# Second-half forms of x written over the used inputs of the output projection, and one combined first step of the feed-forward

## The chip, the cores and the metric

The kernel runs on one core of one Trainium2 chip. The metric is the device time of one execution in microseconds (us), the median of the runs; lower is better. Engines are named as in the profile: PE is the matmul engine (TensorE), PEld its weight loads, DVE the vector engine, ACT the scalar engine, POOL is GpSimd, and SP issues the DMAs.

## The reference

One inference step of a two-layer streaming encoder over 1088 frames (1024 of a new stream, 64 of a running one) with a model width of 1024. Per layer:

```python
h = rms_norm(x, norm_mix_g[layer])
y = even_mixer(h, ...) if layer % 2 == 0 else odd_mixer(h, ...)   # ends in concat(two branches) @ w_out
x = x + y
h = rms_norm(x, norm_ffn_g[layer])
x = x + jnp.square(jax.nn.relu(h @ w_ff1[layer])) @ w_ff2[layer]  # 1024 -> 4096 -> 1024
```

Layer 0 mixes by chunk gating (branch a) and trailing pooling (branch b), layer 1 by a width-31 convolution (branch c) and a gated width-3 convolution (branch d). At the end there is one more rms_norm. All of it is float32.

## The kernel before

Activations lie transposed: x is eight tiles of 128 features by 1088 frames. Every float32 operand of a product is split into a high part (a rounded copy made by ACT, line 165) and a low part (what is left, subtracted by DVE, line 166), and a product is three matmuls: low weight by high data, high by low, high by high. The frames are handled in two halves, c = 0 and c = 1, of 544 frames each, and a half in two quarters of 272.

The two products of the feed-forward are done by a scheme with seven sub-products instead of eight. For it, both the weights and the data are turned into seven **forms** (sums and differences of blocks, each split into a high and a low part). Weight forms are made by `form` (lines 207, 212, then the split) in six buffers W, up to five ahead of their use. Forms of x for one half are made by `forms_of_x` for four row blocks k from x[k] and x[k+4]: two scaled copies on ACT (line 703), five small DVE operations of 272 columns (lines 708, 709, 688, and one split), and three splits of 544 columns. Those of the first half go into the tiles FA, those of the second half into FB.

`last_parts` is the second part of the output projection for one half. For eight tiles m in the order 0, 4, 1, 5, 2, 6, 3, 7 it runs 24 or 48 matmuls (lines 257 to 259), adds the product to x on DVE (line 743), squares x on ACT (line 752) and adds the square to acc on POOL (line 753). With it run steps from the list `beside`, the forms of x among them. For c = 0 they follow their tile; for c = 1 they are collected in `later` and come after the last tile, because FB lies on the side of the memory that still holds the inputs of the output projection (Q, or cc in layer 1): `open_second` gives that side free and takes FB and four work tiles vl from it.

The first product of the feed-forward (`feed_forward`, lines 819 to 821 in `products`) has 16 blocks i of weights. The list STEPS1 takes blocks 0 and 1 for the half c = 0, then blocks 0 and 1 for c = 1, and then each block from 2 to 15 for both halves at once. Each entry of the list is planned with weight forms of its own, so the forms of blocks 0 and 1 are made twice. A step sums its seven sub-products in three pairs of banks (A, B, C; four pairs pp in all): after f = 0, 1, 2 ACT copies a bank out (line 862), after f = 3, 4, 5 DVE adds one (line 865) and scales it (line 858), and after f = 6 DVE scales the last (line 858). The results go to DRAM (hd, line 853) and are read back as forms for the second product (class `Hidden`, line 837). The sum of the result into x is line 901. The order on every engine is set by a scheduler at build time.

Of the kernel before, what the change touches and what calls it, by code (L numbers as in the profile page):

```python
# [11 lines left out]
F32 = mybir.dt.float32  # L12
# [4 lines left out]
P = 128  # L17
# [39 lines left out]
def encoder(ctx, tc, ins, outs):  # L57
# [29 lines left out]
    RIGHT = {"P1", "P2", "t", "raw", "FA", "vr", "sq", "RAW", "e", "cin", "dd", "wide", "r2"}  # L87
    LEFT = {"Q1", "Q2", "FB", "vl", "cc"}

# [14 lines left out]
    def q2(dt=F32R, n=T):  # L104
        return sb([P, n], dt, "Q2", 8)

# [5 lines left out]

    def vl(n=NH):
        return sb([P, n], F32, "vl", 4)

# [222 lines left out]

    STEPS1 = [(0, (0,)), (1, (0,)), (0, (1,)), (1, (1,))] + [(i, (0, 1)) for i in range(2, 16)]


# [9 lines left out]
    def plan_ff(layer):  # L351
        plan(f"f{layer}", None, "stage")
        for s, (i, _) in enumerate(STEPS1):
            src = ins[f"wf1_{layer}"][i].rearrange("p (b c) -> p b c", b=4)
            for f in range(7):
                plan(("f1", layer, s, f), src, "form")
# [65 lines left out]
    for i in range(4):  # L422
        wv.append((q2(n=1024), q2(n=1024)))
        split(*wv[i], wvr[i])
        if i == 0:
            gains(x0[0], *PIECES[0])
# [183 lines left out]
    def pool_out(g, pp):  # L610
        yb[g] = (q2(), q2())
# [17 lines left out]


    ya = []

    def u_tile(m):
        w = take(("u", m))
        ya.append((q1(), q1()))
        for c, (a, b) in enumerate(CH):
            ps = psum()
            n = b - a
            mm3(ps[:, :n], unit_pairs(w, h, c, range(KT)))
            if between and c == 0:  # L640
                between.pop(0)()
            u = tmp()
            dve.tensor_tensor(u[:, :n], ps[:, :n], acc[:, a:b], ALU.mult)
            act.activation(u[:, :n], u[:, :n], AF.Gelu_apprx_tanh)
            dve.tensor_tensor(mix[m][:, a:b], mix[m][:, a:b], u[:, :n], ALU.mult)
            split(ya[m][0][:, a:b], ya[m][1][:, a:b], mix[m][:, a:b])

# [25 lines left out]
    def open_first():  # L673

        open_side("right")
        state["form"] = True
        for k in range(4):
            FF[0, k] = sb([P, 7, 2, NQ], F32R, "FA", 4)

    def open_second():  # L680
        open_side("left")
        vl()
        for k in (3, 2, 0, 1):
            FF[1, k] = sb([P, 7, 2, NQ], F32R, "FB", 4)

# [4 lines left out]
    def forms_of_x(layer, k, c):  # L690
# [5 lines left out]
        def put(f, n, src):  # L696
            t = FF[c, k][:, f : f + n]
            split(t[:, :, 0], t[:, :, 1], src)
# [7 lines left out]
        def first():  # L706
            y1, y2, u, w = b
            dve.tensor_tensor(u[:, 0], y1[:, 0], y1[:, 1], ALU.subtract)
            dve.tensor_tensor(w[:, 0], y2[:, 1], y1[:, 1], ALU.subtract)
            put(0, 1, y1[:, 0:1])  # L710

        def second():
# [8 lines left out]

        return [gains_, first, second, third, lambda: put(5, 2, b[3])]


    def add_out(m, c, w, t, ks):
        a = c * NH
        ps = pair()
        for i in range(2):
            o = a + i * NQ
            mm3(  # L730
                ps[:, i, :NQ],
                [
                    (
                        w[0][:, q * P : (q + 1) * P],
                        w[1][:, q * P : (q + 1) * P],
                        t[0][k][:, o : o + NQ],
                        t[1][k][:, o : o + NQ],
                    )
                    for q, k in ks
                ],  # L740
            )
# [13 lines left out]
    def last_parts(layer, c, weights, t, ks):  # L755

        later = []
        for m in MS:
# [7 lines left out]
        beside.extend(later)  # L766

    load_x(ins["xT"])
    open_psum("f0", 4)
    open_first()  # L770
    begun.add("f0")
    mixed = [t[0] for t in ya + yb], [t[1] for t in ya + yb]
    last_parts(0, 0, lambda m: take(("o0", m)), mixed, [(k, k) for k in (4, 5, 6, 7, 0, 1, 2, 3)])
    for i, m in enumerate(MS):
        add_out(m, 1, take(("o0b", m), 5), mixed, [(k - 4, k) for k in range(4, 8)])
        if i == 1:
            rms_half(0, vr())
    last_parts(0, 1, lambda m: take(("o0a", m), 5), mixed, [(k, k) for k in range(4)])

# [4 lines left out]
    def feed_forward(layer, done):  # L784
# [7 lines left out]

        open_second()
# [4 lines left out]
        def products(key, cs, n, rows):  # L798

# [3 lines left out]
            bank = {}  # L803
            for f, (name, first) in enumerate(
                (("A", True), ("B", True), ("A", False), ("C", True), ("A", False), ("B", False), ("A", False))
            ):
                if first:
                    bank[name] = pair()
                if (*key, f) not in kept:
                    kept[(*key, f)] = take((*key, f), 5)  # L810
                w = kept[(*key, f)]
                for c in cs:
                    ps = bank[name][:, c, :NQ]
                    for q in range(n):
                        lh, ll = w[:, 0, q * P : q * P + P], w[:, 1, q * P : q * P + P]
                        t = FF[c, rows(q, c)][:, PLACE[f]]
                        hi, lo = t[:, 0], t[:, 1]
                        s, e = first and q == 0, q == n - 1
                        pe.matmul(ps, ll, hi, start=s, stop=False, skip_group_check=True)  # L819
                        pe.matmul(ps, lh, lo, start=False, stop=False, skip_group_check=True)  # L820
                        pe.matmul(ps, lh, hi, start=False, stop=e, skip_group_check=True)  # L821
                yield f, bank[name][:, cs[0] : cs[-1] + 1, :NQ]
                aside(2)


        def place(i, c):
            return (3, 2, 0, 1)[i % 4] if c else i % 4

        class Hidden:
# [5 lines left out]
            def form(self, f):  # L835
                t = self.buffer()
                dma.dma_start(out=t, in_=hd[self.i][f])
                for c in range(2):
                    to = FF[c, place(self.i, c)][:, PLACE[f]]
                    split(to[:, 0], to[:, 1], t[:, c * NQ : c * NQ + NQ])  # L840

        factor = acc.rearrange("p (c h t) -> p c h t", c=2, h=2)
        for s, (i, cs) in enumerate(STEPS1):
            last = Hidden(0, vr) if s == len(STEPS1) - 1 else None
            if s == 2:
                aside(len(beside))
            z = {k: halves(vl() if last or s < 2 else vs()) for k in (0, 3, 1, 2)}
            for f, ps in products(("f1", layer, s), cs, 4, lambda q, c: q):
                v = {k: t[:, cs[0] : cs[-1] + 1] for k, t in z.items()}
# [28 lines left out]
                if f == 6:  # L878
# [15 lines left out]
        for j, lo, hi, make, cs in STEPS2 + ENDS[layer]:  # L894
            nxt = [Hidden(i) for i in make]
            part = slice(cs[0], cs[-1] + 1)
            for f, ps in products(("f2", layer, (j, lo)), cs, hi - lo, lambda q, c: place(lo + q, c)):

# [22 lines left out]

    h1 = [[[None] * KT for _ in range(2)] for _ in range(2)]

    def after(j, cs):
        t = sb([P, 7, NH], F32R, "FB", 4)
        places = [t[:, i] for i in range(7)] + [sb([P, NH], F32R, "vl", 4)]

# [215 lines left out]

    cc, means = [], {}


    def ln_steps(c):
# [36 lines left out]
        def finish_(j):  # L1184
            dve.tensor_tensor(ct[j], ct[j], st["r"], ALU.mult)
            act.activation(ct[j], ct[j], AF.Silu, scale=col(O_LG + j), bias=col(O_LB + j))
            split(cc[j][0][:, a:b], cc[j][1][:, a:b], ct[j])

# [9 lines left out]

    open_side("left")
    cc.extend(tuple(sb([P, T], F32R, "cc", 8) for _ in range(2)) for _ in range(4))  # L1200
    load_x(xd)
    dh = [t[0] for t in dd], [t[1] for t in dd]
    for m in MS:
# [8 lines left out]
    begun.add("f1")  # L1212
    mixed = [t[0] for t in cc], [t[1] for t in cc]
    last_parts(1, 0, lambda m: take(("o1c", 0, m), 5), mixed, [(k, k) for k in range(4)])
# [129 lines left out]
```

## Time and profile before

| | |
|---|---|
| median of 3 runs | 2109.45 us (2108.42 to 2110.8) |
| the profiled execution | 2106.23 us, its span 2104.4 us |
| granted clock of PE, mean | 0.983 of full speed |
| PE busy | 2004.5 us (95%) |
| PEld busy | 1969.6 us (94%) |
| DVE busy | 1653.7 us (79%) |
| ACT busy | 965.4 us (46%) |
| POOL busy | 261.5 us (12%) |

PE is busy 95% of the span. In long stretches it never waits; the rest is lost in a few places, mostly at the borders of the stages. So the shares of the whole span say little here, and the profile has to be read by stretches of time and by single waits.

### The profile page before, as it was taken

How to read it: one execution, taken by the hardware profiler on the slowest of the kernel's cores; microseconds unless marked ns; L12 is line 12 of the kernel's file. 1: busy time of each engine (PE TensorE's matmuls, PEld its weight loads, DVE VectorE, ACT ScalarE, POOL GpSimd, SP SyncE). 2: the span in 40 equal slices, each digit the busy share in tenths (PEclk: the TensorE clock that was granted, in tenths of full speed). 3: DMA queues.
4: the chain of work that ended last, by engine and by line, in shares of the span. 5: the costliest groups of instructions: out<-in, count | busy, mean ns of one | idle time of the engine just before them, and what ended most of it. 6: DMA issues, size and time to landing. Idle time of an engine off the chain costs nothing.

```text
span 2104.4 us, 38324 instructions
## 1 busy us (share of the span) xinstructions
PE 2004.5 (95%) x15212; PEld 1969.6 (94%) x15212; DVE 1653.7 (79%) x2755; ACT 965.4 (46%) x1744; POOL 261.5 (12%) x172
## 2 busy tenths in 40 slices
PE   7999998999998999998999989989999999999994
PEld 5799998999998999998999989979999999999994
DVE  7784779666669888878499967898666789888867
ACT  6233555434346444444444425664444455444443
POOL 5200220000000000002176740310000000000003
PEclk9999999999999999999999999989999999999997
DMA  4223224434348444422211132224434366444402
GB/s 153 73 63 104 81 96 145 145 143 145 142 147 273 142 141 147 141 88 96 78 42 41 41 74 83 91 82 160 152 136 153 135 210 211 151 136 151 131 31 86
DMA packets 123029, 254.58 MB, mean 121 GB/s; under 512 B 16672, under 2 KB 35232, under 8 KB 118240
## 3 DMA queue, kind: packets, MB, share of 16 engines
q1 hardware_dynamic: 122848, 252.12, 36.1%
q8 instruction: 119, 1.95, 0.4%
q14 instruction: 62, 0.51, 0.1%
HBM read 180.45 MB, written 71.63 MB: 120 GB/s over the span
## 4 chain that ended last, share of the span: by engine, by line
PE 73%; DVE 17%; ACT 4%; issue 2%; POOL 2%; DMA 2%; DVEq 0%; SPq 0%; ACTq 0%; POOLq 0%
PE pp L819 19%; PE pp L821 19%; PE pp L820 19%; DVE ps L1089 4%; PE pp L257 4%; PE pp L258 3%; PE pp L259 3%; DVE W L166 2%; PE ps L257 2%; PE ps L258 2%; PE ps L259 2%; DVE Wl L166 1%; DVE X L901 1%; DMA vr<-hd 1%; DVE FB L166 1%
## 5 line engine op out<-in xcount | busy, mean ns | idle before, releaser
L819 PE MATMUL pp<-FA,W 128*128 128x272 f32 x1792 | 521.9, 292 | 34.4 <-DVE X L901 25.9
L819 PE MATMUL pp<-FB,W 128*128 128x272 f32 x1792 | 519.6, 290 | 11.6 <-DVE W L166 8.3
L820 PE MATMUL pp<-FA,W 128*128 128x272 f32 x1792 | 519.0, 290 | 1.5 <-DVE FA L166 1.5
L821 PE MATMUL pp<-FA,W 128*128 128x272 f32 x1792 | 518.6, 290 | 0.0
L820 PE MATMUL pp<-FB,W 128*128 128x272 f32 x1792 | 516.6, 288 | 0.0
L821 PE MATMUL pp<-FB,W 128*128 128x272 f32 x1792 | 516.0, 289 | 0.0
L819 PEld LDWEIGHTS pp<-FA,W 128*128 128x128 f32 x1792 | 339.8, 190 | 42.2 <-DVE X L901 30.5
L819 PEld LDWEIGHTS pp<-FB,W 128*128 128x128 f32 x1792 | 338.1, 189 | 14.2 <-issue 7.7
L820 PEld LDWEIGHTS pp<-FA,W 128*128 128x128 f32 x1792 | 342.0, 191 | 1.9 <-DVE FA L166 1.9
L820 PEld LDWEIGHTS pp<-FB,W 128*128 128x128 f32 x1792 | 340.8, 190 | 0.0
L821 PEld LDWEIGHTS pp<-FA,W 128*128 128x128 f32 x1792 | 339.9, 190 | 0.0
L821 PEld LDWEIGHTS pp<-FB,W 128*128 128x128 f32 x1792 | 338.6, 189 | 0.0
L165 ACT ACTIVATE W<-RAW 128x512 fp32r<-128x512 f32 (+3 forms) x324 | 191.1, 595 | 147.3 <-PE pp L821 104.7
L166 DVE TENSOR_TENSOR W<-RAW,W 128x512 fp32r<-128x512 f32 (+3 forms) x324 | 216.3, 670 | 51.9 <-ACT W L165 51.2
L901 DVE TENSOR_TENSOR X<-X,pp 128x544 f32<-128x544 f32 (+1 forms) x280 | 191.4, 690 | 55.1 <-PE pp L821 52.5
L165 ACT ACTIVATE W<-e 128x512 fp32r<-128x512 f32 (+3 forms) x222 | 132.2, 596 | 161.2 <-PE pp L821 118.7
L911 POOL TENSOR_TENSOR acc<-acc,sq 128x544 f32<-128x544 f32 (+1 forms) x24 | 29.6, 1234 | 1367.2 <-ACT sq L910 1367.2
L166 DVE TENSOR_TENSOR W<-e,W 128x512 fp32r<-128x512 f32 (+3 forms) x222 | 146.0, 658 | 61.7 <-ACT W L165 61.1
L258 PE MATMUL pp<-FB,Wh 128*128 128x272 f32 x640 | 186.4, 291 | 0.0
L257 PE MATMUL pp<-FB,Wl 128*128 128x272 f32 x480 | 140.1, 292 | 3.8 <-DVE X L1120 2.3
L1078 POOL TENSOR_TENSOR X<-X,X 128x1118 f32<-128x1118 f32 x46 | 130.0, 2827 | 106.2 <-ACT X L1076 103.3
L259 PE MATMUL pp<-FB,Wh 128*128 128x272 f32 x480 | 139.3, 290 | 0.0
(238 smaller groups left out, 3768.1 us busy)
## 6 DMA issues: line engine op xcount, KB each, us to landing
RAW<-in_wf SPq DMA_DIRECT2D x62, 1024.0 KB, 5.2
vr<-hd SPq DMA_DIRECT2D x119, 272.0 KB, 2.9
hd<-vl SPq DMA_DIRECT2D x105, 272.0 KB, 2.3
vl<-hd SPq DMA_DIRECT2D x105, 272.0 KB, 2.8
hd<-vr SPq DMA_DIRECT2D x91, 272.0 KB, 2.3
raw<-in_wi SPq DMA_DIRECT2D x18, 512.0 KB, 3.4
hd<-vl SPq DMA_DIRECT2D x42, 136.0 KB, 1.8
X<-in_xT SPq DMA_DIRECT2D x8, 544.0 KB, 3.8
```

The lines of the kernel that those rows point to most:

```text
L165: act.activation(hi, src, AF.Copy)
L166: dve.tensor_tensor(lo, src, hi.bitcast(F32), ALU.subtract)
L257: pe.matmul(ps, ll, rh, start=s, stop=False)
L258: pe.matmul(ps, lh, rl, start=False, stop=False)
L259: pe.matmul(ps, lh, rh, start=False, stop=e)
L819: pe.matmul(ps, ll, hi, start=s, stop=False, skip_group_check=True)
L820: pe.matmul(ps, lh, lo, start=False, stop=False, skip_group_check=True)
L821: pe.matmul(ps, lh, hi, start=False, stop=e, skip_group_check=True)
L901: dve.tensor_tensor(t, t, ps, ALU.subtract if f in (1, 4, 6) else ALU.add)
L911: (dve if j == 3 else gp).tensor_tensor(at, at, sq, ALU.add)
L1078: return gp.tensor_tensor(o, o, t, ALU.add)
L1089: return dve.scalar_tensor_tensor(out=o, in0=z[:, k : k + NO], scalar=wk(k), in1=o, op0=ALU.mult, op1=ALU.add)
```

## The change

The side of the memory that holds Q is no longer closed and reopened. Its tiles Q1, Q2, Q3 stay, and other things are written over them:

- The inputs `ya` of the output projection are kept per half of the frames, each tile with its high and low part side by side. Splits into them that cross the border of the halves become two (`split_halves`).
- The forms of x's second half are written over the parts of `ya` and `yb` that have been used up (`form_at`, `pair_at`, `one_at`): blocks k = 0 and 1 over the inputs of branch b, k = 2 over the first half of `ya`, k = 3 over its second half, which is used until the last tile. So for c = 1 the steps of k = 0, 1 and all but one of k = 2 follow their tile as for c = 0, and only the last step of k = 2 and those of k = 3 come after the last tile. The step that splits f = 0 now is the last of a block.
- The four work tiles vl are the halves of the two tiles Q3.
- The first product takes block 0 for both halves, one behind the other: the sub-products f of c = 1 follow those of c = 0 by three (`APART`). All other blocks take both halves at once. The weight forms of blocks 0 and 1 are made once, and during block 0 only up to two are made ahead.
- In layer 1, `ya` takes the place of cc, and the inputs of layer 1's first products and the second half of the hidden forms lie in the same places.

```diff
@@ def forms_of_x
+        def put(f, n, src):
+            t = form_at(c, k, f, n)
             split(t[:, :, 0], t[:, :, 1], src)
...
-        return [gains_, first, second, third, lambda: put(5, 2, b[3])]
+        return [gains_, first, second, third, lambda: put(5, 2, b[3]), lambda: put(0, 1, b[0][:, 0:1])]
@@ def form_at
+    pair_at = [[quads(t.rearrange("p (f n) -> p f n", f=2)) for g in gs for t in yb[g]][a : a + 3]
+               for gs, a in (((3, 2, 1), 0), ((3, 2, 1), 3))]
+    pair_at += [[quads(ya[m][c]) for m in range(3)] for c in range(2)]
+    one_at = [quads(ya[3][c])[:, i : i + 1] for c in range(2) for i in range(2)]
+    def form_at(c, k, f, n=1):
+        if c == 0:
+            return FF[k][:, f : f + n]
+        if f == 0:
+            return one_at[k]
+        i = (f - 1) % 2
+        return pair_at[k][(f - 1) // 2][:, i : i + n]
@@ def last_parts
-                (beside if c == 0 else later).extend(forms_of_x(layer, m - 4, c))
+                steps = forms_of_x(layer, m - 4, c)
+                if c == 1 and m == 6:
+                    beside.extend(steps[:-1])
+                    later.append(steps[-1])
+                else:
+                    (later if c == 1 and m == 7 else beside).extend(steps)
@@ def feed_forward
-    STEPS1 = [(0, (0,)), (1, (0,)), (0, (1,)), (1, (1,))] + [(i, (0, 1)) for i in range(2, 16)]
+        TOGETHER = [(f, (0, 1)) for f in range(7)]
+        APART = [(f - c * 3, (c,)) for f in range(10) for c in range(2) if 0 <= f - c * 3 < 7]
-        for s, (i, cs) in enumerate(STEPS1):
+        for i in range(16):
...
-            for f, ps in products(("f1", layer, s), cs, 4, lambda q, c: q):
+            for f, cs, ps in products(("f1", layer, i), TOGETHER if i else APART, 4, range(4), 5 if i else 2):
...
-                if s == 1 and f == 1:
+                if i == 0 and f == 3 and cs == (0,):
                     rms_half(1, square_tile())
```

What this does to the order on the engines is shown at the end of layer 0's output projection. On DVE before, where the tiles m = 3 (X_1778) and m = 7 (X_1786) are added to x, there are weight forms between the additions, and the forms of the second half (FB) come behind the last one:

```order
L743 TENSOR_TENSOR X_1784<-X_1784,pp_2783 128x544
L166 TENSOR_TENSOR W_2812<-RAW_2711,W_2812 128x512
L743 TENSOR_TENSOR X_1778<-X_1778,pp_2815 128x544
L166 TENSOR_TENSOR W_2845<-RAW_2711,W_2845 128x512
L743 TENSOR_TENSOR X_1786<-X_1786,pp_2848 128x544
L166 TENSOR_TENSOR W_2918<-e_2712,W_2918 128x512
L166 TENSOR_TENSOR FB_2894<-vr_2934,FB_2894 128x272
```

On DVE now, at the same place, the same two tiles are X_1786 and X_1794 (lines are 23 further on, L766 is the addition, L177 the low part, L734, L735 and L714 the small operations of the forms):

```order
L766 TENSOR_TENSOR X_1792<-X_1792,pp_2822 128x544
L177 TENSOR_TENSOR Q_222_1362<-vr_2809,Q_222_1362 128x2x272
L177 TENSOR_TENSOR Q_261_1683<-vr_2804,Q_261_1683 128x272
L177 TENSOR_TENSOR W_2858<-RAW_2732,W_2858 128x512
L734 TENSOR_TENSOR vr_2891<-vr_2887 128x272
L766 TENSOR_TENSOR X_1786<-X_1786,pp_2861 128x544
L735 TENSOR_TENSOR vr_2892<-vr_2889,vr_2887 128x272
L714 SCALAR_TENSOR_TENSOR vr_2891<-vr_2891,vr_2889 128x272
L177 TENSOR_TENSOR Q_234_1457<-vr_2889,Q_234_1457 128x2x272
L223 TENSOR_TENSOR RAW_2732<-RAW_2732 128x512
L714 SCALAR_TENSOR_TENSOR vr_2892<-vr_2891,vr_2889 128x272
L766 TENSOR_TENSOR X_1794<-X_1794,pp_2905 128x544
```

Three of the four blocks of forms have moved ahead of the last addition.

On ACT before, at the last square (sq from X_1786), the copy of the first bank of the feed-forward (vl from pp_2916) stands behind that square:

```order
L165 ACTIVATE W_2918<-e_2712 128x512
L165 ACTIVATE FB_2894<-vr_2934 128x272
L752 ACTIVATE sq_2874<-X_1786 128x544
L165 ACTIVATE FB_2894<-vr_2936 128x2x272
L862 ACTIVATE vl_2912<-pp_2916 128x272
L165 ACTIVATE W_2945<-RAW_2711 128x512
```

On ACT now (L775 is the square, L900 the copy, into a half of a Q3 tile, L729 the scaled copies for block k = 3):

```order
L176 ACTIVATE Q_250_1580<-vr_2892 128x2x272
L775 ACTIVATE sq_2936<-X_1794 128x544
L900 ACTIVATE Q_367_2619<-pp_2965 128x272
L729 ACTIVATE vr_2981<-X_1786,par_62 128x544
L729 ACTIVATE vr_2983<-X_1794,par_62 128x544
L900 ACTIVATE Q_367_2619<-pp_2987 128x272
L176 ACTIVATE Q_235_1458<-vr_2983 128x2x272
L176 ACTIVATE Q_262_1684<-vr_2981 128x272
```

The copy still stands behind the last square, and the forms of k = 3 now stand where those of k = 0 stood.

## Rows read from the trace of the kernel before

**Rows 1.** Busy time by stretch: us, then PE, PEld, DVE, ACT, POOL, granted clock, DMA.

```profile
276.00:294.00 18.00, 18.00 (x146) 18.00 (x145) 14.77 (x20) 8.40 (x13) 9.11 (x6) 1.00 0.28 110
294.00:312.00 18.00, 15.20 (x115) 14.28 (x113) 17.58 (x34) 15.16 (x31) 1.50 (x2) 1.00 0.25 83
312.00:316.00 4.00, 4.00 (x20) 4.00 (x21) 3.88 (x8) 3.33 (x8) 0.00 (x0) 0.57 0.31 104
316.00:336.00 20.00, 13.51 (x96) 12.13 (x96) 19.09 (x40) 10.95 (x22) 0.00 (x0) 1.00 0.29 102
```

**Rows 2.** Timeline: start, duration, engine, line; first matmuls and last scalings of steps.

```profile
294.05 0.28 PE L819 MATMUL pp<-FA,W 128*128 128x272 f32 x1
...
294.25 0.72 DVE L743 TENSOR_TENSOR X<-X,pp 128x544 f32<-128x544 f32 x1 [1.67 <-PE pp L259]
...
372.24 0.72 DVE L858 SCALAR_TENSOR_TENSOR vr<-pp,acc 128x544 f32<-128x544 f32 x1
393.26 0.72 DVE L858 SCALAR_TENSOR_TENSOR vr<-pp,acc 128x544 f32<-128x544 f32 x1
...
1371.53 0.29 PE L819 MATMUL pp<-FA,W 128*128 128x272 f32 x1
...
1475.42 0.72 DVE L858 SCALAR_TENSOR_TENSOR vl<-pp,acc 128x544 f32<-128x544 f32 x1
```

**Rows 3.** Waits of PE from 294 to 345 us: total, times, longest.

```profile
PE pp L819 <- DVE W L166: 4.3, 2, 2.8
PE pp L819 <- ACT vl L862: 2.1, 2, 1.7
PE pp L819 <- DVE vl L858: 1.8, 1, 1.8
```

**Rows 4.** Waits of PE from 1371 to 1430 us.

```profile
PE pp L819 <- DVE W L166: 4.0, 2, 2.8
PE pp L819 <- ACT vl L862: 3.6, 2, 3.0
```

**Rows 5.** Timeline of DVE at 298 and 301 us, without waits.

```profile
298.30 0.68 DVE L166 TENSOR_TENSOR W<-RAW,W 128x512 fp32r<-128x512 f32 x1
298.90 0.71 DVE L166 TENSOR_TENSOR FB<-vr,FB 128x544 fp32r<-128x544 f32 x1
299.53 0.68 DVE L166 TENSOR_TENSOR W<-RAW,W 128x512 fp32r<-128x512 f32 x1
...
301.12 0.43 DVE L865 TENSOR_TENSOR vl<-vl,pp 128x272 f32<-128x272 f32 x1
301.47 0.43 DVE L709 TENSOR_TENSOR vr<-vr,vr 128x272 f32<-128x272 f32 x1
```

**Rows 6.** Timeline of POOL and DVE at 1333 us: a sum of squares beside small operations.

```profile
1333.57 1.63 POOL L753 TENSOR_TENSOR acc<-acc,sq 128x544 f32<-128x544 f32 x1 [3.01 <-ACT sq L752]
...
1333.89 1.60 DVE L708 TENSOR_TENSOR vr<-vr 128x272 f32<-128x272 f32 x1
1335.42 0.43 DVE L709 TENSOR_TENSOR vr<-vr,vr 128x272 f32<-128x272 f32 x1
```

**Rows 7.** Timeline of DVE and PE: layer 1's additions, first and eighth of c = 0, first of c = 1.

```profile
1320.88 0.72 DVE L743 TENSOR_TENSOR X<-X,pp 128x544 f32<-128x544 f32 x1 [1.70 <-PE pp L259]
...
1348.35 0.71 DVE L743 TENSOR_TENSOR X<-X,pp 128x544 f32<-128x544 f32 x1
...
1351.58 1.19 PE L312 MATMUL pp<-acc,ones 128*128 128x272 f32 x4 [3.55 <-POOL acc L753]
...
1355.66 0.71 DVE L743 TENSOR_TENSOR X<-X,pp 128x544 f32<-128x544 f32 x1
```

**Rows 8.** Timeline of ACT and PE behind layer 1's last addition.

```profile
1376.13 0.66 ACT L752 ACTIVATE sq<-X 128x544 f32<-128x544 f32 x1 [0.60 <-POOL acc L753]
...
1377.24 0.38 ACT L862 ACTIVATE vl<-pp 128x272 f32<-128x272 f32 x1
...
1377.67 0.59 PE L819 MATMUL pp<-FA,W 128*128 128x272 f32 x1 [2.96 <-ACT vl L862]
```

More of the change, by code (lines that the diff above doesn't have):

```diff
@@ L111, in vr, with open_vl, vl @@
         return sb([P, n], F32, "vr", 4)
-    def vl(n=NH):
-        return sb([P, n], F32, "vl", 4)
+    left = []
+    def open_vl():
+        left.clear()
+        left.extend(t[:, a : a + NH] for t in (q3(F32), q3(F32)) for a in (0, NH))
+    def vl():
+        left.append(left.pop(0))
+        return left[-1]
     turn = [0]
@@ L352, in plan_ff @@
         plan(f"f{layer}", None, "stage")
-        for s, (i, _) in enumerate(STEPS1):
+        for i in range(16):
             src = ins[f"wf1_{layer}"][i].rearrange("p (b c) -> p b c", b=4)
             for f in range(7):
-                plan(("f1", layer, s, f), src, "form")
+                plan(("f1", layer, i, f), src, "form")
         steps = {(j, a): b for j, a, b, _, _ in STEPS2 + ENDS[layer]}
@@ L422, in encoder @@
     for i in range(4):
-        wv.append((q2(n=1024), q2(n=1024)))
+        wv.append(tuple((q3 if i == 3 else q2)(n=1024) for _ in range(2)))
         split(*wv[i], wvr[i])
@@ L610, in pool_out @@
     def pool_out(g, pp):
-        yb[g] = (q2(), q2())
+        yb[g] = tuple((q2 if g else q3)() for _ in range(2))
         for c, (a, b) in enumerate(CH):
@@ L628, in encoder, with split_halves @@
     between.append(lambda: pool_out(0, parts[0]))
+    def split_halves(t, src, a, b):
+        for c in range(2):
+            lo, hi = max(a, c * NH), min(b, c * NH + NH)
+            if lo < hi:
+                split(*(t[c][:, i, lo - c * NH : hi - c * NH] for i in range(2)), src[:, lo:hi])
     ya = []
@@ L634, in u_tile @@
         w = take(("u", m))
-        ya.append((q1(), q1()))
+        ya.append([sb([P, 2, NH], F32R, "Q1", 8) for _ in range(2)])
         for c, (a, b) in enumerate(CH):
@@ L763, in last_parts, with columns, mixed @@
             if m >= 4:
-                (beside if c == 0 else later).extend(forms_of_x(layer, m - 4, c))
+                steps = forms_of_x(layer, m - 4, c)
[4 more added lines that the diff above has]
+                    (later if c == 1 and m == 7 else beside).extend(steps)
         aside(len(beside))
         beside.extend(later)
+    def columns(c, i):
+        return slice(c * NH + i * NQ, c * NH + i * NQ + NQ)
+    def mixed(part, k, c, i):
+        if k < 4:
+            return ya[k][c][:, part, i * NQ : i * NQ + NQ]
+        return yb[k - 4][part][:, columns(c, i)]
     load_x(ins["xT"])
@@ L784, in feed_forward, with products @@
     def feed_forward(layer, done):
-        open_second()
         hd = [drp.tile([7, P, NH], F32, tag=f"hd{layer}_{i}", name=f"hd{layer}_{i}") for i in range(16)]
         kept = {}
-        def products(key, cs, n, rows):
+        TOGETHER = [(f, (0, 1)) for f in range(7)]
+        APART = [(f - c * 3, (c,)) for f in range(10) for c in range(2) if 0 <= f - c * 3 < 7]
+        def products(key, order, n, rows, depth=5):
             bank = {}
[L804 to L807, printed above, removed]
+            for f, cs in order:
+                name, first = (("A", 1), ("B", 1), ("A", 0), ("C", 1), ("A", 0), ("B", 0), ("A", 0))[f]
+                if name not in bank:
                     bank[name] = pair()
                 if (*key, f) not in kept:
-                    kept[(*key, f)] = take((*key, f), 5)
+                    kept[(*key, f)] = take((*key, f), depth)
                 w = kept[(*key, f)]
@@ L815, in products @@
                         lh, ll = w[:, 0, q * P : q * P + P], w[:, 1, q * P : q * P + P]
[L816 removed]
+                        t = form_at(c, rows[q], PLACE[f])[:, 0]
                         hi, lo = t[:, 0], t[:, 1]
                         s, e = first and q == 0, q == n - 1
[L819 removed]
+                        pe.matmul(ps, ll, hi, start=bool(s), stop=False, skip_group_check=True)
                         pe.matmul(ps, lh, lo, start=False, stop=False, skip_group_check=True)
                         pe.matmul(ps, lh, hi, start=False, stop=e, skip_group_check=True)
[L822 removed]
+                yield f, cs, bank[name][:, cs[0] : cs[-1] + 1, :NQ]
                 aside(2)
[L826 to L827 removed]
         class Hidden:
@@ L838, in form @@
                 for c in range(2):
-                    to = FF[c, place(self.i, c)][:, PLACE[f]]
+                    to = form_at(c, self.i % 4, PLACE[f])[:, 0]
                     split(to[:, 0], to[:, 1], t[:, c * NQ : c * NQ + NQ])
         factor = acc.rearrange("p (c h t) -> p c h t", c=2, h=2)
-        for s, (i, cs) in enumerate(STEPS1):
-            last = Hidden(0, vr) if s == len(STEPS1) - 1 else None
-            if s == 2:
+        for i in range(16):
+            last = Hidden(0, vr) if i == 15 else None
+            if i == 1:
                 aside(len(beside))
-            z = {k: halves(vl() if last or s < 2 else vs()) for k in (0, 3, 1, 2)}
-            for f, ps in products(("f1", layer, s), cs, 4, lambda q, c: q):
+            z = {k: halves(vl() if last or i == 0 else vs()) for k in (0, 3, 1, 2)}
+            for f, cs, ps in products(("f1", layer, i), TOGETHER if i else APART, 4, range(4), 5 if i else 2):
                 v = {k: t[:, cs[0] : cs[-1] + 1] for k, t in z.items()}
@@ L896, in feed_forward @@
             part = slice(cs[0], cs[-1] + 1)
-            for f, ps in products(("f2", layer, (j, lo)), cs, hi - lo, lambda q, c: place(lo + q, c)):
+            order = [(f, cs) for f in range(7)]
+            for f, _, ps in products(("f2", layer, (j, lo)), order, hi - lo, [k % 4 for k in range(lo, hi)]):
                 m, h = ((j, 0), (j + 4, 1), (j, 1), (j, 0), (j + 4, 1), (j, 1), (j + 4, 0))[f]
@@ L922, in encoder @@
     h1 = [[[None] * KT for _ in range(2)] for _ in range(2)]
+    rest = []
     def after(j, cs):
-        t = sb([P, 7, NH], F32R, "FB", 4)
-        places = [t[:, i] for i in range(7)] + [sb([P, NH], F32R, "vl", 4)]
+        if j == 0:
+            rest.extend(t[:, a : a + NH] for t in (q3(), q3()) for a in (0, NH))
+        flat = lambda t: t.rearrange("p f h t -> p f (h t)")
+        places = [flat(form_at(1, j, f))[:, 0] for f in range(7)] + [rest.pop()]
         def one(k, c):
@@ L1142, in short_conv @@
         project(("db", j), gate_b, RD)
-    cc, means = [], {}
+    means = {}
     def ln_steps(c):
@@ L1196, in encoder @@
         short_conv(j)
-    open_side("left")
-    cc.extend(tuple(sb([P, T], F32R, "cc", 8) for _ in range(2)) for _ in range(4))
     load_x(xd)
-    dh = [t[0] for t in dd], [t[1] for t in dd]
+    dh = lambda part, k, c, i: dd[k][part][:, columns(c, i)]
     for m in MS:
@@ L1212, in encoder @@
     begun.add("f1")
-    mixed = [t[0] for t in cc], [t[1] for t in cc]
+    open_vl()
     last_parts(1, 0, lambda m: take(("o1c", 0, m), 5), mixed, [(k, k) for k in range(4)])
```

27 lines of the change are left out of this document (11 added, 16 removed).

## The prediction

> **What bounds the kernel now.** The page's first part says PE 95% busy, so PE's path sets the time and only its idle time and its slow clock can be won. I went next to the busy time by stretch, to find where PE is not full: in the last pass of layer 0's output projection it is (18.00 of 18.00 us), and in the three stretches behind 294 us it is not, while DVE works 17.58 of 18, 3.88 of 4 and 19.09 of 20 us [rows 1]. So there DVE is the bound. Full PE runs 146 matmuls in 18.00 us, about 0.125 us each, and an output tile of 24 takes 3.0 us.
>
> Then the timeline, for the price of that border. A full step of the feed-forward, 168 matmuls, takes 393.26 - 372.24 = 21.02 us [rows 2], again 0.125 each. Layer 0 starts its first product at 294.05 and ends its third step's work (blocks 0, 1 and 2, both halves) at 372.24: 78.2 us for 63.06 us of matmuls, so 15.1 are lost. Layer 1 ends a fourth step at 1475.42 from 1371.53: 103.9 for 84.1, 19.8 lost. These two stretches are what the change touches; some 1.3 us in each are the matmuls of rms_norm and the last result's latency, which stay.
>
> The waits of PE say for what: in layer 0 4.3 us for the low part of a weight form, 2.1 for a copy by ACT, 1.8 for a scaling on DVE [rows 3]; in layer 1 4.0 and 3.6 [rows 4]. The rest are many short waits and the clock: after idle time it was granted 0.57 of full, so the lower of 1.2 and 2.4 GHz, for most of 312 to 316, in which PE ran 20 matmuls where 32 fit [rows 1]. That stretch cost about 1.6 us.
>
> **What is removed.** The weight forms of blocks 0 and 1 are made once, 7 steps of c = 1 for each block fewer: 14 forms a layer. On DVE each costs a low part at a pitch of .60 us (298.30 to 298.90, [rows 5]) and, for four of seven forms, a sum at the same size: 14 x .60 + 8 x .60 = 13.2 us a layer. ACT loses 14 rounded copies, SP two loads. As DVE is full behind the border, this comes off the waits there, and the two longest of each layer (2.8 and 2.8, both for a weight form) should go.
>
> **What is moved.** The forms of blocks k = 0, 1 and most of 2 for the second half run among the last tiles. The pitches are .63 us for a low part of 544 columns (298.90 to 299.53) and .35 for one of 272 (301.12 to 301.47) [rows 5]. In this stretch PE cannot be slower than its 3.0 us a tile, but DVE now must do, between the second tile's addition and the eighth's: 7 additions and 7 splits of 544 at .635, 8 weight operations at .60, 13 small ones at .35 = 18.25 us. PE gives it 6 x 3.0 = 18 us. On top comes POOL. A sum of squares lasts 1.63 us there, and a DVE operation beside it took 1.60 in place of .43: 1.17 more [rows 6]. Six of them make 7.0. So DVE ends 18.25 + 7.0 - 18 = 7.2 us behind where it ended on time before (294.25, 1.67 us after waiting for PE [rows 2]).
>
> The trace has a check on this: layer 1's c = 0 pass already carries just this load. Its first addition is at 1320.88 and on time, its eighth at 1348.35 [rows 7]: 27.47 us for seven tiles of 3.0, so 6.5 us behind. I take 7.
>
> The Trainium skill, SBUF — State Buffer, section "SBUF: two separate sides", has a rule that speaks against this change: the port pair that DVE and GpSimd share is locked for a whole instruction, and the one that comes second stands still until it is done. The trace agrees in kind, with 1.17 us of delay beside 1.63 us of POOL [rows 6]; held for the whole of 1.63 in all six cases, DVE would be 2.8 us later in each layer, and the sum would come out near 2104.
>
> **What a late DVE costs, layer 0.** The first copy of a bank by ACT stands behind the last square in ACT's order, and the square behind the last addition. That addition starts at 294.25 + 7 = 301.2; it, the square and the copy take about .7, .6 and .4, so the copy is done at 302.9. PE needs that bank copied before the sub-product f = 2 of c = 0 can overwrite it. PE is there at 294.05 + 24 x .125 = 297.05, so it waits 5.8 us, a new wait. It then runs two more products (3.0), loses about 2 to the low clock (taken from the 1.6 of [rows 1], with one more such dip) and needs 1.15 for rms_half and 2.6 for further matmuls. The next thing it may lack is the low part of k = 3, f = 0. DVE reaches it 17 operations after the last addition: 3 x .60 + 6 x .635 + 8 x .35 = 8.4, one POOL sum at 1.0, and 1.4 for the addition itself and for waits, at 312.0, where PE stands at 311.6. That is .4 more. Loss: 5.8 + .4 + 2 = 8.2, with .5 for the small rest and the 1.3 that stay 10.0, against 15.1. Gain 5.1 us.
>
> What is behind k = 3 is not late: DVE then has only one weight form for each 3.0 us of PE, or 1 us of work. During block 0 forms are made only two ahead, 6 us of matmuls; a form's chain is a sum, a copy and a low part, about .65 each, so cover stands unless DVE's own queue holds it. The eight splits that become two at the halves' border lie in a stretch in which PE is full; with DVE at 79% I cost them at nothing, and at 8 x .35 = 2.8 if that cover is gone.
>
> **Layer 1.** The first addition of c = 1 stays at 1355.66 [rows 7]; it is late already, since PE itself waited 3.55 for POOL. To the seventh addition DVE has 16 operations of 544 (10.2), 8 x .60, 10 x .35 = 18.5, with 5 POOL sums 5.2 and about 1 of waits, so that it starts at 1380.4. Here ACT's copy stands behind the seventh square, so it is done 1.6 later, at 1382.0. Before, it started at 1377.24 and PE, which could have gone on at 1371.53 + 3.0, resumed at 1377.67 after a wait of 2.96 [rows 8]. Now PE waits to 1382.0, 7.5 in all. Beyond that DVE has 7 more operations of 544, 10 small ones, 4 x .60, two POOL sums and 1.4 for copies until the weight form f = 5 of block 0, which comes at 1394.5. Its product ends at 1396.0; without any wait it would at 1371.5 + 92 x .125 + 1.15 = 1384.2. So 11.8 are lost, with .5 and 1.3 as above 13.6, against 19.8: gain 6.2.
>
> **Sum.** 2106.23 - 5.1 - 6.2 = 2094.9 for the profiled execution. Its time stands 3.2 below the median of 2109.45, so the runs should show 2098.
>
> **Bounds.** The unknown is how much POOL holds DVE up. At no delay the lag of DVE is about 0 in layer 0, as before [rows 2]; PE then loses some 3.7 in layer 0 (two clock dips, rms and latency) and 7.5 in layer 1, where ACT is late already: gains of 11.4 and 12.3, as a median 2085.7. At the other end a lag twice the measured 6.5.
>
> **Rivals.**
> - DVE keeps up. For it: many POOL sums may fall beside operations that read the product banks, and such additions in [rows 7] show .71 or .72, none prolonged. Against it: the 6.5 us lag under the same load. Time 2086 to 2091. Chance 0.18.
> - The waits only move. The third block's forms, the squares and the first block's copies all fall together, the idle of 8 us brings several clock dips of 1.6 us, and the two ahead-made weight forms run out, say two waits of 2.8 as [rows 3] has them. Gains of 5.1 + 6.2 shrink to nothing: 2105 to 2113. Chance 0.19. For it: DVE does no less work before the copy of bank A than before, only the work behind it is less.
> - Slower, from one mechanism: the lag at ACT's first copy. The loss in layer 0 is about the lag + 3.0, so it passes the 15.1 of before at a lag of 12.1 us. That is where each POOL sum holds up two DVE operations (6 more x 1.17 = 7.0 on 7). Layer 0 then loses 17.0, and layer 1, 7 us later too, 20.6: 2106.23 + 1.9 + .8, with two more dips at 1.6, is 2112.1, so 2115 as a median. Against it: [rows 6] shows the next operation at .43 again. Chance 0.13.
>
> My forecast has 0.50. A change of 0.2%, 4.2 us, is about what a measurement of this kernel can tell from none. Faster beyond it are the forecast (its own range 2093 to 2104) and the first rival, together 0.68; the second rival is the 0.19 of the same; slower the 0.13 of the third. The range of 2087 to 2110 leaves out about 0.1 at either side.
>
> **What would show it.** In the changed profile the last addition of layer 0's c = 1 stands about 7 us behind PE's last output tile; PE waits about 5 us for ACT's copy at f = 2 of block 0, and 7 in layer 1; the waits of 2.8 for a weight form are gone in layer 0 and small in layer 1; behind block 0 PE is full. The forecast is wrong if PE waits under 2 us at that copy, if it waits over 10, or if the second border, into the second product, moves by more than 3 us, which I cost at nothing.

## The result, and the profile after

| | before | after |
|---|---|---|
| median | 2109.07 us (2108.42 to 2110.8, 4 runs) | 2097.74 us (2094.83 to 2099.91, 4 runs) |
| the profiled execution | 2106.23 us | 2099.91 us |
| DVE busy | 1653.7 us | 1630.4 us |
| ACT busy | 965.4 us | 948.0 us |

The ratio is 0.9944, with an interval of 0.9927 to 0.9961: faster, by 11.3 us at the medians, where 11.3 were forecast. The profiled execution is the slowest of its four and shows only 6.3 us, so what follows counts the two borders by themselves.

The stretches of [rows 1], in the kernel after (us, PE, PEld, DVE, ACT, POOL, granted clock, DMA):

```profile
276.00:294.00 18.00, 18.00 (x146) 18.00 (x145) 17.62 (x25) 12.58 (x21) 6.11 (x4) 1.00 0.30 111
294.00:312.00 18.00, 12.47 (x79) 11.89 (x77) 18.00 (x30) 11.38 (x23) 4.67 (x3) 0.81 0.03 8
312.00:316.00 4.00, 4.00 (x32) 4.00 (x33) 3.45 (x8) 1.61 (x4) 0.00 (x0) 1.00 0.39 113
316.00:336.00 20.00, 20.00 (x160) 19.80 (x159) 14.66 (x31) 9.28 (x18) 0.00 (x0) 1.00 0.49 175
```

DVE now is full ahead of the border (17.62 of 18 us, 14.77 before). PE stands idle or slow for one stretch, with 79 matmuls in 18 us, and from 312 us on it is full again with 32 in 4.00 and 160 in 20.00, where it had 20 and 96. DVE drops to 14.66 of 20 there, since the second set of weight forms is gone.

The first matmuls and last scalings that answer to [rows 2], with the last matmul of the output projection of layer 0 at the head:

```profile
293.55 0.29 PE L270 MATMUL pp<-Q,W 128*128 128x272 f32 x1
293.69 0.28 PE L861 MATMUL pp<-FA,W 128*128 128x272 f32 x1
...
366.60 0.72 DVE L896 SCALAR_TENSOR_TENSOR vr<-pp,acc 128x544 f32<-128x544 f32 x1
387.63 0.72 DVE L896 SCALAR_TENSOR_TENSOR vr<-pp,acc 128x544 f32<-128x544 f32 x1
...
1370.94 0.28 PE L861 MATMUL pp<-FA,W 128*128 128x272 f32 x1
...
1465.69 0.72 DVE L896 SCALAR_TENSOR_TENSOR Q<-pp,acc 128x544 f32<-128x544 f32 x1
```

In layer 0 the three blocks take 366.60 - 293.69 = 72.9 us, 9.8 over the 63.06 of their matmuls (15.1 before). In layer 1 four take 94.75, 10.7 over 84.08 (19.8 before). So the borders gave 5.3 and 9.1 us. Some of the 9.1 had been lost just ahead of the first matmul, as shown below.

PE's waits from 294 to 345 us, then from 1371 to 1430 us (total, times, longest), against [rows 3] and [rows 4]:

```profile
PE pp L861 <- ACT Q L900: 5.5, 1, 5.5
```

```profile
PE pp L861 <- ACT Q L900: 4.1, 1, 4.1
PE pp L861 <- DVE Q L903: 1.1, 1, 1.1
PE pp L323 <- POOL acc L776: 1.0, 1, 1.0
```

No weight form is waited for any more. One wait for ACT's first copy has come in each layer. Its chain in layer 0, with the POOL sums ahead of it:

```profile
277.32 1.44 POOL L776 TENSOR_TENSOR acc<-acc,sq 128x544 f32<-128x544 f32 x1 [29.29 <-ACT sq L775]
281.51 1.42 POOL L776 TENSOR_TENSOR acc<-acc,sq 128x544 f32<-128x544 f32 x1 [2.75 <-ACT sq L775]
285.57 1.63 POOL L776 TENSOR_TENSOR acc<-acc,sq 128x544 f32<-128x544 f32 x1 [2.64 <-ACT sq L775]
289.67 1.62 POOL L776 TENSOR_TENSOR acc<-acc,sq 128x544 f32<-128x544 f32 x1 [2.46 <-ACT sq L775]
294.29 1.38 POOL L776 TENSOR_TENSOR acc<-acc,sq 128x544 f32<-128x544 f32 x1 [3.00 <-ACT sq L775]
298.03 1.70 POOL L776 TENSOR_TENSOR acc<-acc,sq 128x544 f32<-128x544 f32 x1 [2.36 <-ACT sq L775]
```

```profile
277.92 1.14 DVE L735 TENSOR_TENSOR vr<-vr,vr 128x272 f32<-128x272 f32 x1 [0.38 <-ACT vr L729]
...
281.62 1.89 DVE L177 TENSOR_TENSOR Q<-vr,Q 128x544 fp32r<-128x544 f32 x1
...
285.90 1.60 DVE L734 TENSOR_TENSOR vr<-vr 128x272 f32<-128x272 f32 x1
287.43 0.42 DVE L735 TENSOR_TENSOR vr<-vr,vr 128x272 f32<-128x272 f32 x1
...
290.00 1.59 DVE L714 SCALAR_TENSOR_TENSOR vr<-vr,vr 128x272 f32<-128x272 f32 x1
...
294.37 1.85 DVE L177 TENSOR_TENSOR W<-RAW,W 128x512 fp32r<-128x512 f32 x1
...
298.46 1.82 DVE L223 TENSOR_TENSOR RAW<-RAW 128x512 f32<-128x512 f32 x1
...
300.55 0.71 DVE L766 TENSOR_TENSOR X<-X,pp 128x544 f32<-128x544 f32 x1
```

```profile
301.39 0.64 ACT L775 ACTIVATE sq<-X 128x544 f32<-128x544 f32 x1
301.94 0.38 ACT L900 ACTIVATE Q<-pp 128x272 f32<-128x272 f32 x1
```

```profile
302.37 0.59 PE L861 MATMUL pp<-FA,W 128*128 128x272 f32 x1 [5.53 <-ACT Q L900]
```

Beside each of these six POOL sums one DVE operation is held up. Operations that take .43 to .71 us elsewhere take 1.14 us beside the first sum and 1.59 to 1.89 beside the others. The last addition starts at 300.55, 6.7 us after PE's last output tile had ended (293.84); in the kernel before it started as that tile ended [rows 2]. The square follows it, then the copy, then PE. In layer 1, PE's wait for POOL ahead of the last pass, then the eighth addition of c = 0 and the first and the seventh of c = 1, and the copy:

```profile
1349.50 2.18 PE L323 MATMUL pp<-acc,ones 128*128 128x272 f32 x4 [4.17 <-POOL acc L776]
```

```profile
1345.95 0.71 DVE L766 TENSOR_TENSOR X<-X,pp 128x544 f32<-128x544 f32 x1
...
1352.34 0.71 DVE L766 TENSOR_TENSOR X<-X,pp 128x544 f32<-128x544 f32 x1
...
1376.40 0.71 DVE L766 TENSOR_TENSOR X<-X,pp 128x544 f32<-128x544 f32 x1
```

```profile
1377.77 0.38 ACT L900 ACTIVATE Q<-pp 128x272 f32<-128x272 f32 x1
```

The first addition, held fixed at 1355.66 in the forecast [rows 7], now starts at 1352.34, since the whole pass ahead of it runs earlier: the eighth addition of c = 0 went from 1348.35 to 1345.95. PE's first product came only .6 us earlier, for PE lost time on the way to it. It waited 4.17 us for POOL's last sum of c = 0, where it had waited 3.55, and ran behind that at a granted clock of 0.60 (1349 to 1356 us; 1.00 there before). From the start of that wait to the first product it took 25.6 us (1345.33 to 1370.94), where it had taken 23.5 (1348.03 to 1371.53). These 2.1 us lie ahead of the first matmul, so the loss of 10.7 does not count them.

### The profile page after: what moved, and what is told of

Same layout as the page of the kernel before. It is cut to its first block, busy times and chain, and to the rows that moved or that the text cites. A ratio compares the mean times of both kernels' runs of the same rounds, so it can differ in the third digit from the quotient of the medians.

```text
span 2098.1 us, 38092 instructions
## 1 busy us (share of the span) xinstructions
PE 2006.6 (96%) x15212; PEld 1974.7 (94%) x15212; DVE 1630.4 (78%) x2697; ACT 948.0 (45%) x1710; POOL 261.7 (12%) x172
## 4 chain that ended last, share of the span: by engine, by line
PE 74%; DVE 17%; issue 2%; ACT 2%; POOL 2%; DMA 2%; DVEq 0%; SPq 0%; ACTq 0%; POOLq 0%
PE pp L861 20%; PE pp L863 20%; PE pp L862 19%; DVE ps L1131 4%; PE pp L268 3%; PE pp L269 3%; PE pp L270 3%; PE ps L268 2%; PE ps L269 2%; PE ps L270 2%; DVE Q L177 1%; DVE Wl L177 1%; DVE W L177 1%; DVE X L940 1%; DVE X L1173 1%
## 5 line engine op out<-in xcount | busy, mean ns | idle before, releaser
L861 PE MATMUL pp<-Q,W 128*128 128x272 f32 x1792 | 518.7, 290 | 2.0 <-DVE Q L903 1.1
L862 PE MATMUL pp<-Q,W 128*128 128x272 f32 x1792 | 516.9, 289 | 1.0 <-DVE Q L177 1.0
L863 PE MATMUL pp<-Q,W 128*128 128x272 f32 x1792 | 517.1, 289 | 0.0
L862 PEld LDWEIGHTS pp<-Q,W 128*128 128x128 f32 x1792 | 340.3, 190 | 1.5 <-DVE Q L177 1.4
L861 PEld LDWEIGHTS pp<-Q,W 128*128 128x128 f32 x1792 | 338.9, 189 | 2.9 <-DVE X L940 1.4
L863 PEld LDWEIGHTS pp<-Q,W 128*128 128x128 f32 x1792 | 339.1, 189 | 0.0
L176 ACT ACTIVATE W<-RAW 128x512 fp32r<-128x512 f32 (+3 forms) x308 | 182.4, 595 | 150.5 <-PE pp L863 108.5
L177 DVE TENSOR_TENSOR W<-RAW,W 128x512 fp32r<-128x512 f32 (+3 forms) x308 | 204.7, 666 | 56.5 <-ACT W L176 55.7
L268 PE MATMUL pp<-Q,Wl 128*128 128x272 f32 x768 | 226.1, 294 | 12.8 <-DVE X L1181 10.4
L269 PE MATMUL pp<-Q,Wh 128*128 128x272 f32 x768 | 224.7, 293 | 0.0
L270 PE MATMUL pp<-Q,Wh 128*128 128x272 f32 x768 | 224.0, 292 | 0.0
L176 ACT ACTIVATE W<-e 128x512 fp32r<-128x512 f32 (+3 forms) x210 | 124.6, 593 | 158.6 <-PE pp L863 127.4
L177 DVE TENSOR_TENSOR W<-e,W 128x512 fp32r<-128x512 f32 (+3 forms) x210 | 136.9, 652 | 66.5 <-ACT W L176 66.2
L268 PEld LDWEIGHTS pp<-Q,Wl 128*128 128x128 f32 x768 | 147.9, 193 | 14.6 <-DVE X L1181 11.0
```

The lines of the kernel that those rows point to most:

```text
L176: act.activation(hi, src, AF.Copy)
L177: dve.tensor_tensor(lo, src, hi.bitcast(F32), ALU.subtract)
L268: pe.matmul(ps, ll, rh, start=s, stop=False)
L269: pe.matmul(ps, lh, rl, start=False, stop=False)
L270: pe.matmul(ps, lh, rh, start=False, stop=e)
L861: pe.matmul(ps, ll, hi, start=bool(s), stop=False, skip_group_check=True)
```

## The experiments

Two questions: is the gain the saved weight forms or the early forms of x, and is what is left set by DVE and POOL, or by ACT's order? The loss named below is, as above, the time from the first matmul to the last scaling of three blocks in layer 0 (four in layer 1), less their matmuls.

**The changed kernel again.**

> The changed kernel once more, for a second profile. My theory: a new wait of 5 to 6 us for ACT's first copy in layer 0 and of 4 to 5 in layer 1 appears again at the same product, since it comes from the order and DVE's load. What differed by 1.5 to 4.4 us between the first two profiles far from the border (into the second product of both layers) is either repeated here, and then belongs to the change, or not, and then it is the spread of single runs. Time 2095 to 2100 us.

2098.90 us, ratio 0.9959 (0.9947 to 0.997). Losses 9.9 and 12.1, waits for the copy 5.5 and 4.2, so the new waits belong to the change. Far from the border the two profiles of the same kernel differ by 1.3 to 6 us in a stage. Yet three stretches are longer than before in both: the way into the second product, by 1.5 and .2 us in layer 0 and by 4.3 and 1.5 in layer 1, and the way from layer 0's second product to layer 1's first, by 3.5 and 1.4. Of these last, 2.1 and 1.3 are the wait for POOL and the slow clock behind it that were told above. Whether the rest is a price of the change or the spread of single runs stays open.

**Forms of x early, weight forms twice.**

> The changed kernel with the old list: the second half's forms of x stay early, over the used inputs, but blocks 0 and 1 are taken for c = 0 and then for c = 1 and their weight forms are made twice. Theory (the gain is DVE work saved behind the border, the 14 weight forms a layer, 13.2 us of DVE): about 2106 us (2102 to 2110), with waits for weight forms (DVE W) of 2 us and more back between 294 and 340 us. Rival (the gain is the early forms): 2096 to 2100 and no such waits.

```diff
+    STEPS1 = [(0, (0,)), (1, (0,)), (0, (1,)), (1, (1,))] + [(i, (0, 1)) for i in range(2, 16)]
...
-            for f, cs, ps in products(("f1", layer, i), TOGETHER if i else APART, 4, range(4), 5 if i else 2):
+            for f, cs, ps in products(("f1", layer, s), [(f, ics) for f in range(7)], 4, range(4), 5):
```

2108.88 us, ratio 1.0011 (1.0002 to 1.002): no gain, if anything a small loss. PE's waits in layer 0, then in layer 1:

```profile
PE pp L862 <- ACT Q L901: 6.4, 3, 5.6
PE pp L862 <- DVE Q L897: 1.0, 1, 1.0
```

```profile
PE pp L862 <- ACT Q L901: 6.0, 3, 4.2
PE pp L862 <- DVE W L177: 2.7, 2, 1.5
PE pp L862 <- DVE Q L897: 1.0, 1, 1.0
```

The wait for the copy is there as in the changed kernel, and behind it more waits and 13.9 and 16.5 us of loss. The expected wait for weight forms came in layer 1 alone. The early forms by themselves are not the gain. The borders of this profile lose 4.5 us less than before, which the medians do not show. The same profile lost more than that in the stretches named under the changed kernel's second profile: the way into the second product is 1.1 and 5.3 us longer than before, and the way from the wait for POOL to layer 1's first product 1.9 longer.

**Forms late, first attempt.**

> The changed kernel with all forms of x's second half again behind the last output tile, as before, and weight forms of blocks 0 and 1 made once. Theory that both parts are needed (c = 1 of block 0 starts 6 us after c = 0, while DVE needs some 18 us for the four blocks of forms and the weight forms between them): about 2113 us (2106 to 2118), with a wait for the low part of a form of x of 8 us or more in each layer. Rival (the 14 saved weight forms are the gain wherever the forms of x stand): 2096 to 2101.

```diff
-                if c == 1 and m == 6:
+                if False:
...
-                    (later if c == 1 and m == 7 else beside).extend(steps)
+                    (later if c == 1 else beside).extend(steps)
```

2096.89 us, ratio 0.9949 (0.9937 to 0.9961). It is not the experiment that was meant: in this version the first products of c = 1 stand ahead of part of the forms that they read, so they use old data and wait for nothing, and the scheduler still drew some forms ahead of the last additions. What it does show: with those forms taken off PE's path, PE waits 5.4 and 6.0 us for the copy all the same.

**Forms late, in order.**

> The changed kernel with the forms of x's second half queued on DVE behind the last addition of x, as they stood before, and finished ahead of the first product of c = 1; weight forms of blocks 0 and 1 made once. Theory that both parts are needed (c = 1 of block 0 starts 6 us after c = 0, while DVE needs some 18 us for the four blocks and the weight forms between them): 2106 to 2118 us, with waits of 8 us or more a layer ahead of c = 1's first product. Rival (the 14 saved weight forms are the gain wherever the forms of x stand): 2096 to 2101.

```diff
+                (later if c == 1 else beside).extend(steps)
...
+        def behind(step):
+            with tc.issue_after(added.ins):
+                step()
...
                 if i == 0 and f == 3 and cs == (0,):
+                    aside(len(beside))
```

2100.83 us, ratio 0.9969 (0.9958 to 0.9981). My theory expected 2106 to 2118 and failed. PE's waits in layer 0:

```profile
PE pp L863 <- DVE Q L177: 2.1, 4, 0.8
PE pp L862 <- ACT Q L176: 0.5, 2, 0.4
```

There is no wait of 8 us, but a row of short ones, since DVE makes the forms one block after the other and PE follows it; losses 11.8 and 13.3. So making the weight forms once brings 6.7 us with the forms of x as late as ever. Placing them early brings another 2 to 3 by the medians; the intervals of the ratios overlap (0.9958 to 0.9981 here, 0.9927 to 0.9961 and 0.9947 to 0.997 with early forms), so that this part is not clear of the noise.

**The copy ahead, first attempt.**

> The changed kernel with the squares of the tiles m = 3 and m = 7 of c = 1 issued later (behind the products f = 2 and f = 3 of block 0, rms_half behind f = 5), so that in layer 0 ACT's first copy no longer stands behind the last square; in layer 1 it stands where it stood. Theory (DVE's lag is the limit, ACT's place in line only shows it): the wait for the copy falls from 5.5 to about 2 us and a wait for the low part of block k = 3's form f = 0 takes its place, since DVE makes that one at 310.4 as before; the time is within 1.5 us of the changed kernel. Rival (the order on ACT costs it): 3 us less, 2094 to 2095.

```diff
+            if c == 1 and m in (3, 7):
+                late_squares.append(lambda m=m: add_squares(m, c))
...
+                if i == 0 and f in (2, 3) and cs == (0,):
+                    late_squares.pop(0)()
```

2098.93 us, ratio 0.9957 (0.994 to 0.9973). It tells nothing: the copy (at 303.64 us) then stood behind two splits and a scaled copy, ahead of which ACT had waited 1.5 us for DVE, and PE's wait was 5.6 us.

**The copy ahead of all that waits for the last tiles.**

> The changed kernel with ACT's first copy of block 0 ahead of the last two squares of c = 1 and of the forms k = 2 and 3, in both layers. Theory (DVE's load up to the last form is the limit): the wait for the copy falls from 5.5 to under 2.5 us in layer 0, and a wait of PE for a low part of a form of x takes its place; the time is within 2 us of the changed kernel's 2098.9. Rival (the place in ACT's queue costs it): 5 us less in layer 0 and 4 in layer 1, 2090.

```diff
+                (late if c == 1 and m >= 6 else beside).extend(steps)
...
+                if i == 0 and f == 0 and cs == (0,):
+                    with tc.issue_after(copied.ins):
+                        while late:
+                            late.pop(0)()
```

2097.28 us, ratio 0.9958 (0.9945 to 0.9972): no different from the changed kernel. Layer 0's first two waits:

```profile
PE pp L861 <- DVE Q L909: 2.8, 1, 2.8
PE pp L861 <- ACT Q L900: 2.5, 2, 2.3
```

3 us of the wait for ACT became 2.8 for DVE, not for a low part, as expected, but for an addition of the feed-forward (L909) that stands behind the forms in DVE's queue. Losses 10.2 and 10.7. In layer 1 PE still waited 4.5 us for the copy, so only layer 0 tells the two apart. There ACT's order only showed the lag.

**No sums on POOL.**

> The changed kernel without POOL's additions of squares to acc in the passes for c = 1 (14 in all; the squares of seven of the eight tiles are left out of the sum). Theory (POOL holds DVE up by 1.17 us each time): no DVE operation of 0.4 to 0.7 us lasts over 1.2 us there, the last addition comes 6 to 7 us earlier, PE's wait for the first copy is under 1.5 us in layer 0, and the time is 2088 to 2092. If POOL's sums are not the cause: 2097 to 2100.

```diff
-            gp.tensor_tensor(at, at, sq, ALU.add)
+            if c == 0:
+                gp.tensor_tensor(at, at, sq, ALU.add)
```

This kernel leaves out the squares of seven of the eight tiles of c = 1. 2084.07 us, ratio 0.9888 (0.9875 to 0.9901), beyond the 2088 to 2092 expected. The last addition of layer 0, and the stretch behind the border:

```profile
295.77 0.71 DVE L766 TENSOR_TENSOR X<-X,pp 128x544 f32<-128x544 f32 x1
```

```profile
294.00:312.00 18.00, 18.00 (x138) 17.37 (x137) 16.80 (x34) 12.22 (x26) 0.00 (x0) 1.00 0.21 72
```

The addition stands .35 us behind the first product's first matmul (295.42 in this run), where it was 6.9 behind (300.55 against 293.69). PE is full at the full clock; losses 2.3 and 3.4. So POOL's 14 sums of c = 1 cost the changed kernel 14 us: the delay itself, and the low clock that the idle time brought.

**The sums on DVE.**

> The changed kernel with the squares of c = 1 added to acc on DVE in place of POOL (7 additions of 544 columns a layer). Theory: DVE pays .635 for each in place of 1.17 of delay, so its lag is 3.7 us shorter, PE's wait for the first copy falls from 5.5 to about 2 us, and the time to 2092 to 2095. If POOL's delay overlaps with waits that are there anyway: 2098 to 2103.

```diff
+            (dve if c else gp).tensor_tensor(at, at, sq, ALU.add)
```

2095.59 us, ratio 0.9939 (0.9926 to 0.9952): just above the 2092 to 2095 expected, and by the intervals not to be told from the changed kernel. Layer 0 gave what was expected (loss 6.3 against 9.8), layer 1 nothing (12.0). There the waits were spread over copies, low parts and the sum itself, 4.7 us in all, and the granted clock was 0.51 from 1380 to 1390 us. Why they came there, I did not settle.

**The sums on PE.** Squares rounded by ACT to the high-part format, and summed by one-pass matmuls with ones.

> The changed kernel with the squares of x summed on PE (one-pass matmuls with ones into a pair of banks, two for each tile, in all four passes) in place of POOL and of rms_half's matmuls; POOL does nothing in these passes. Theory (POOL's sums hold DVE up and so cost 14 us of the changed kernel, and some 4 more where PE waits for POOL in layer 1): 16 x .125 = 2.0 us of matmuls a pass less 1.15 for rms_half, so 3.4 us more PE work over four passes; 2098 - 14 - 4 + 3.4 = 2083 us (2080 to 2088). If PE then waits for the squares: 2090 and more.

```diff
+    def sum_up():
+        while waiting:
+            c, sq, s, e = waiting.pop(0)
+            for i in range(2):
+                pe.matmul(total[c][:, i, :NQ], ones_r, halves(sq)[:, i], start=s, stop=e, skip_group_check=True)
...
+        sq = sb([P, NH], F32R, "sq", 1)
+        act.activation(sq, xm, AF.Square)
+        waiting.append((c, sq, m == 0, m == 7))
```

2082.46 us, ratio 0.9888 (0.9873 to 0.9902), against 2083 expected: 15 us faster than the changed kernel, and the best one here. Behind the border:

```profile
294.00:312.00 18.00, 18.00 (x142) 17.62 (x141) 16.77 (x33) 12.38 (x25) 0.00 (x0) 1.00 0.14 48
```

Losses 1.6 and 1.5. Between 1340 and 1371 us the changed kernel's wait for POOL (4.2, at L323) has become this:

```profile
PE pp L174 <- ACT sq L785: 1.6, 1, 1.6
```

**The sums on PE, forms late.**

> The same, and the forms of x's second half queued behind the last addition. Theory (POOL ate the gain of the early forms: without its delay DVE has the time among the last tiles that the early forms need): 8 us or more slower than the one with early forms, about 2093 to 2101. If the place of the forms hardly matters, as with POOL's sums (about 3 us): 2084 to 2088.

The edit is that of the forms late, in order, on top. 2098.58 us, ratio 0.9949 (0.9936 to 0.9962), losses 10.8 and 10.6. Without POOL's sums the early place of the forms is worth 16 us, with them 2 to 3.

**The kernel before, with the sums on PE.**

> The kernel before the change with the squares of x summed on PE in the same way. Theory (POOL's delay counts where DVE is full at the last tiles, which before the change was the case in layer 1's pass for c = 0 alone; there PE waits 3.55 us for POOL): 3 to 8 us faster than the kernel before, 2100 to 2105, so that the change is worth some 20 us without POOL's sums and 10 with them. Rival (POOL's delay costs the kernel before as much as the one after): 2090 to 2096.

The same edit on the kernel before. 2102.32 us, ratio 0.9979 (0.997 to 0.9988), as the theory had it: 5.4 us for the kernel before, 15 for the one after. Its losses are 13.4 and 12.5 (15.1 and 19.8 before), so that most of what it gains lies in layer 1. Without POOL's sums the change brings 20 us, with them 10.

## Why the prediction was right

- **The new wait of layer 0**: 5.8 us forecast, 5.5 measured; the lag of the last addition 7.0 and 6.7 (300.55 against PE's last tile at 293.8); the loss 10.0 and 9.8; the gain 5.1 and 5.3. Six operations were held up, by .7 to 1.2 us each, 6.5 in all, for the 7.0 reckoned. PE then waited for no form of k = 3 (.4 reckoned).
- **Layer 1**: the loss was 13.6 forecast and 10.7 and 12.1 measured, the wait 7.5 and 4.1. The term that was mis-sized is the start of the ledger. The first addition was reckoned 15.9 us ahead of PE's first product, as before (1355.66 and 1371.53), and stood 18.6 ahead (1352.34 and 1370.94). Of these 2.7 us only .6 is DVE's; 2.1 is PE, which was late itself after its wait for POOL and the slow clock. Counted with these 2.1 (1.3 in the second profile), layer 1's border gave 7.0 and 6.4 us, for the 6.2 forecast. Two smaller slips in the ledger nearly cancel: five POOL sums stand at 5.2, where 1.17 each makes 5.9, and the eight sub-products up to f = 5 are 96 matmuls and not 92, .5 us.
- **The sum** came out at the median to 0.3 us, and to 0.9 in the second set of runs. That is partly luck. In the profiles the borders gave 14.4 and 12.9 us, for 11.3 forecast, and other stretches, which the forecast put at nothing, took some 8 back in either; the profiled execution was forecast at 2094.9 and took 2099.91.
- **The signs of being wrong**: PE's wait at the copy lay within the 2 to 10 us given. The second border, allowed 3 us, moved by 1.5 and 4.3 us in the first profile, which in layer 1 is beyond it, and by .2 and 1.5 in the second. That it costs nothing is not shown.
- **What is removed** held: the waits for weight forms are gone, and taking the blocks once is 6.7 of the 9 to 11 us (forms late, in order).
- **The rivals.** That DVE keeps up failed in the changed kernel and is what happens without POOL's sums (2084.07, a little below the 2086 to 2091 given for it). The bound with no delay by POOL put the losses at 3.7 and 7.5; they were 2.3 and 3.4. That the waits only move, and that POOL holds up two operations, did not come: one operation per sum is held. Nor did the hold-up for the whole of 1.63 us, with a sum near 2104: the five that fell in full were 1.14 to 1.18.
- **A theory that was wrong, if not one of the prediction**: that both parts of the change need each other. It was argued ahead of the runs with the forms late, and forms left late cost only 2 to 3 us more than early ones, because POOL takes back nearly all that the early place gives (16 us without POOL's sums).

## What to carry to other kernels

When work moves into a stretch in which one engine has time to spare, count what another engine does to that time: here half the gain went to seven small POOL operations a pass, which cost DVE some 1.17 us each, though in layer 0 PE waited for none of them. Look for the check in the same trace, a stretch that already carries the load to come; the lag of 6.5 us read there forecast the 6.7 of the new place. And a wait that names one engine (ACT's copy) can be the queue of another: moving the copy moved only the name of the wait, while moving the load removed it.

## What the runs showed of the hardware

- A DVE operation with both inputs in SBUF beside a POOL sum (1.38 to 1.70 us in layer 0's last pass) took 1.59 to 1.89 us instead of .43 to .71, by 1.14 to 1.18 us wherever it fell in full, and the next was at its own duration again. Additions that read a product bank were not held up (.71 or .72), even when they lay wholly beside a sum. In layer 1 the DVE operation behind such an addition then had the rest of the delay, 1.27 us for the .72 that L327 takes at 310.77:

```profile
1356.39 1.37 POOL L776 TENSOR_TENSOR acc<-acc,sq 128x544 f32<-128x544 f32 x1 [6.95 <-ACT sq L775]
```

```profile
1356.45 0.71 DVE L766 TENSOR_TENSOR X<-X,pp 128x544 f32<-128x544 f32 x1
1357.07 1.27 DVE L327 SCALAR_TENSOR_TENSOR vr<-vr,acc 128x544 f32<-128x544 f32 x1
```

- POOL is held up too. Its sum lasts 1.38 us where a DVE operation with both inputs in SBUF still has .15 us to run as the sum starts (at 294.29), 1.63 where it has .41 (285.57), and 1.70 where it has .51 (298.03); an addition from a product bank with .40 to run leaves it at 1.37 (1372.63 us in the kernel before). So the 1.63 us of [rows 6] hold some .25 in which POOL, by this estimate, waited for DVE.
- PE's idle time of 5.5 us at layer 0's border cost more than its length: the granted clock was 0.81 of full from 294 to 312 us, and matmuls that issue every .125 us at the upper of its two levels came every .23 us for 3.9 us (302.8 to 306.6), at the lower one: 1.7 us lost. With the wait gone the stretch ran at 1.00.
